# The first fourteen operands of a quarter-block product loaded straight into their remainder tiles

## The chip, the cores and the metric

The kernel runs on one core of a Trainium2 chip, as one program. The metric is the device time of one execution in microseconds (us). Three executions of the kernel before are shown, and one more under the profiler; all times of engines and queues come from that profiled one.

## What is computed

One layer of a hybrid decoder for a sequence of 2048 tokens of width 1024, in fp32. The part that matters here is its second half, an MLP of hidden width 4096 between two residual steps:

```python
h = x * (1.0 + sc2) + sh2
f = jnp.square(jax.nn.relu(h @ w_mlp_in[l])) @ w_mlp_out[l]
x = _layer_norm(DEEPNORM_ALPHA * x + (1.0 + g2) * f, ln2_g[l], ln2_b[l])
```

The first half (a gated causal convolution, a multi-scale pooling, an output projection and a norm) comes ahead of it and isn't touched.

## The kernel before, in words

**Precision.** Every fp32 operand is cut in two: a high part in fp32r, written by ScalarE (`split`, L86), and a remainder, the operand minus its high part, written by VectorE (L87). A product takes three matmuls, high by high, high by remainder and remainder by high (`mm3`, L91 to L93). So no operand can be multiplied before both `split` instructions on it are done, ScalarE's first.

**Blocks.** The 2048 rows are worked in two halves (`b` = 0 and 1) of `T` = 1024. Large products are made by the seven-product scheme on 2 by 2 blocks. In `mlp`, `up` runs over eight groups `g` of 512 hidden channels; the left operands of all of them are the same 14 pieces `B`, kept in 28 tiles of the tag `h` (high part and remainder of each), while the weights come through tiles of the tags `r` and `w`. Each of the seven products of a group reads two pieces of `B`, that is, four `h` tiles. The results of a group are stored to DRAM (`usum`). `down` then multiplies them with the second weight, in steps over products and halves of the groups.

**The quarter-block product.** For `b` = 1 (`DEEPER`) one of `down`'s seven products, A12 by B21, is split once more into seven products of quarter blocks. Its left operands are `usum[g, 1]` and the sums of its quarters, `udeep[g]`; its right operands are `wdeep[g]`, the weight's quarters and their sums. All of these lie in DRAM by then: `wdeep` is written while `up` runs (`sum_deep`, L972), `usum` and `udeep` at the end of each group (`closed`, L1060). `deep_operands(g)` (L1204) loads four pieces for each of the eight groups: 128x1024 of `usum` into an `r` tile, 128x1024 of `wdeep` into a `w` tile, 128x768 of `udeep` into an `r` tile and 128x768 of `wdeep` into a `w` tile. Each is then split into two `h` tiles. `deep_matmuls` (L1219) makes 42 matmuls of 128x256 for each group: seven products (`DEEP`), two row tiles, three passes. In a group the first of the seven reads the pieces 0 and 1, the second already the pieces 2 and 3. `left.pop()` (L1267) makes, between the third and the fourth group of operands, the sums that were put off for the last group of `up`; it takes one `h` tile for `s4`, and the stores of `usum` and `udeep` for group 7 follow it.

**Tiles.** The tag `h` has 28 tiles, `r` has 5, `w` has 6, all of 128x1024 and 4 bytes. A tile is given out when its first writer is due, and comes free when its last reader is done. At the end of `up`, `r` and `w` tiles still hold weights of the last group, and all 28 `h` tiles hold `B`: those of a piece come free with the product that reads it last.

**Order.** The kernel doesn't set semaphores. Its instructions are ordered for each engine and each queue when it is built, by a planner that goes by the order in which they are written, by the tiles that are free, and by its own costs; the order then stands, and an engine or a queue that waits for one instruction takes none behind it. Loads go through SP's queue (`nc.sync.dma_start`), most stores through POOL's.

The lines that the change and the prediction speak of: L86 and L87 (`split`), L91 to L93 (`mm3`), L1011, L1067 and L1071 (stores of `usum` and `udeep`), L1084 and L1086 (loads of the next step of `down`), L1204 to L1213 (`deep_operands`), L1219 (`deep_matmuls`), L1232 to L1250 (`deep_sums`), L1263 to L1276 (their order).

Of the kernel before, what the change touches and what calls it, by code (L numbers as in the profile page):

```python
# [8 lines left out]
F32 = mybir.dt.float32  # L9
# [20 lines left out]
Q = 256  # L30
QUARTERS = slice(0, 256), slice(256, 512)
DEEPER = (1,)
DEEP_SUMS = (0,), (1,), (2,), (3,), (4, 5), (6, 7), (), ()
HALF_SUMS = (1, 2, 3, 3, 3, 3, 3, 0)
WARM = (5, 3, 1, 2, 2, 2)
# [13 lines left out]
def tile_hybrid_layer(ctx: ExitStack, tc: tile.TileContext, opening, xT, x, wada, win,  # L49
# [13 lines left out]
    def mk(p, shape, dt, tag, bufs):  # L63
        names[0] += 1
        return p.tile(shape, dt, name=f"{tag}_{names[0]}", tag=tag, bufs=bufs)

    def t_h(dt=F32R):
        return mk(big, [P, T], dt, "h", 28)
# [4 lines left out]
    def t_w(dt=F32R):  # L73
        return mk(big, [P, T], dt, "w", 6)
# [10 lines left out]
    def split(src, hi, lo):  # L85
        high = nc.scalar.copy(hi, src)  # L86
        return high.ins, nc.vector.tensor_tensor(lo, src, hi.bitcast(F32), op=ALU.subtract).ins  # L87
# [7 lines left out]
    def tt(out_, a, b_, op):  # L95
        return nc.vector.tensor_tensor(out_, a, b_, op=op)  # L96
# [875 lines left out]
    def sum_deep(g):  # L972
        a, e = t_o(T), t_o(T)
        nc.sync.dma_start(a, w2[g, 2])
        b11, b12, b21, b22 = (a[:, i * Q : i * Q + Q] for i in range(4))
        t2, t3, t4 = (e[:, i * Q : i * Q + Q] for i in range(3))
        tt(t3, b22, b12, ALU.subtract)
        tt(b12, b12, b11, ALU.subtract)
        tt(t2, b22, b12, ALU.subtract)
        tt(t4, b21, t2, ALU.subtract)  # L980
        nc.gpsimd.dma_start(wdeep[g][:, :T], a)
        nc.gpsimd.dma_start(wdeep[g][:, T:], e[:, : 3 * Q])
# [6 lines left out]
    def up(b, g, B):  # L989
# [62 lines left out]
        nc.scalar.activation(c21, c21, AF.Square)  # L1052
        if b not in DEEPER:
            tt(c11, c21, c11, ALU.subtract)
# [59 lines left out]
    def down(b, F, g2, close):  # L1114
        X, Y = {}, {}
        lo_, hi_ = halves
        closing = b + 1 == NB
        deeper = b in DEEPER
        steps = [(i, hf) for i in ((1, 0) if deeper else (0, 1)) + (2, 3, 5, 4, 6) for hf in range(2)]
# [84 lines left out]
        def deep_operands(g):  # L1204
            tiles = []
            for t, src, n in ((t_r, usum[g, 1], T), (lambda: t_w(F32), wdeep[g][:, :T], T),
                              (t_r, udeep[g], 3 * Q), (lambda: t_w(F32), wdeep[g][:, T:], 3 * Q)):
                r = t()
                nc.sync.dma_start(r[:, :n], src)
                hi, lo = t_h(), t_h()  # L1210
                split(r[:, :n], hi[:, :n], lo[:, :n])
                tiles.append((hi, lo))
            return tiles  # L1213
# [49 lines left out]
        if deeper:  # L1263
            tiles = {}
            for g in range(3):
                tiles[g] = deep_operands(g)
            left.pop()(t_h(F32))  # L1267
            banks = []
            for gs, ns in (((g,), range(7)) for g in range(NC)):
                for g in gs:  # L1270
                    if g + 3 < NC and g + 3 not in tiles:
                        tiles[g + 3] = deep_operands(g + 3)
                if gs[-1] == NC - 1:
                    ready = operands(2)
                deep_matmuls(banks, gs, tiles, ns)
            deep_sums(banks)  # L1276
        else:
            ready = operands(0)
# [116 lines left out]
    def mlp(b, B, back, g2):  # L1395
# [15 lines left out]
        for g in range(NC):  # L1411
# [4 lines left out]
            del sums[:HALF_SUMS[g]]  # L1416
            if b in DEEPER:
                for n in DEEP_SUMS[g]:
                    sum_deep(n)
# [69 lines left out]
```

## Time and profile before

| | |
|---|---|
| time, median of 3 runs (lowest to highest) | 1735.71 us (1734.92 to 1739.76) |
| the profiled execution's own time | 1735.93 us |
| its span, first to last instruction | 1734.2 us |
| mean granted TensorE clock | 0.999 of full speed |
| TensorE busy, matmuls | 1724.6 us, 99% |
| weight loads, beside them | 1436.3 us, 83% |
| VectorE busy | 1313.6 us, 76% |
| ScalarE busy | 868.4 us, 50% |
| DMA, mean over the span | 268 GB/s |

A share over 1700 us says little about a change to one stage. Matmuls are pipelined, so where TensorE loses time is read from the distance between the starts of two matmuls, and from what the profile says each waited for. For the queues and the other engines the order of time in the stage counts: when a load was issued and when its data were there, when a split could start, and what the engine did before.

### The profile page before, as it was taken

The numbers are of one execution on the slowest core, as the hardware profiler recorded it, in microseconds if no ns is written. First come the engines' busy times: TensorE is split into PE (matmuls) and PEld (weight loads), VectorE is DVE, ScalarE is ACT, GpSimd is POOL, SyncE is SP. The second block draws the span as 40 slices with busy tenths as digits, with TensorE's granted clock in tenths as the row PEclk, the third lists the DMA queues.
The fourth block names the chain that finished last, engine by engine and source line by source line (L and its number), as shares of the span: only waits on it lengthen the run. The fifth ranks groups of instructions, "written<-read, shape, count | busy, mean of one in ns | idle before, by whom it ended". The sixth has DMA issues, their size and how long they took to land.

```text
span 1734.2 us, 21910 instructions
## 1 busy us (share of the span) xinstructions
PE 1724.6 (99%) x7855; PEld 1436.3 (83%) x7855; DVE 1313.6 (76%) x1726; ACT 868.4 (50%) x1172; POOL 205.0 (12%) x399
## 2 busy tenths in 40 slices
PE   9999999999999999999999999999999999999998
PEld 8888888888888888888888888888888889888887
DVE  8897798877777676759686789697566759665796
ACT  6322358554454554436573345765445567444451
POOL 0222220122322000100000000102111110000000
PEclk9999999999999999999999999999999999999999
DMA  9998777778888998887572265657545579777771
GB/s 387 345 340 318 300 268 269 257 268 330 317 326 317 384 419 328 309 279 278 191 266 85 99 232 217 226 190 283 205 177 221 209 260 418 308 281 258 253 265 49
DMA packets 142685, 465.24 MB, mean 268 GB/s; under 512 B 16488, under 2 KB 17008, under 8 KB 142576
## 3 DMA queue, kind: packets, MB, share of 16 engines
q1 hardware_dynamic: 97920, 303.39, 47.8%
q0 software_dynamic: 44656, 160.46, 24.3%
q8 instruction: 61, 1.00, 0.2%
q14 instruction: 48, 0.39, 0.1%
HBM read 318.55 MB, written 145.23 MB: 267 GB/s over the span
## 4 chain that ended last, share of the span: by engine, by line
PE 97%; DMA 1%; DVE 1%; issue 0%; ACT 0%; DVEq 0%; SPq 0%; ACTq 0%
PE ps L92 31%; PE ps L91 31%; PE ps L93 31%; PE ps L423 3%; DMA w<-wdeep 1%; PE ps L771 1%; DVE h L87 0%; PE ps L147 0%; DVE h L198 0%; PE ps L125 0%; ACT h L86 0%; DVE o L96 0%; DVE o L1359 0%; DVE o L1365 0%; DVEq L1485 0%
## 5 line engine op out<-in xcount | busy, mean ns | idle before, releaser
L92 PE MATMUL ps<-h,w 128*128 128x512 f32 x1312 | 510.3, 389 | 0.0
L93 PE MATMUL ps<-h,w 128*128 128x512 f32 x1312 | 510.1, 389 | 0.0
L91 PE MATMUL ps<-h,w 128*128 128x512 f32 x1312 | 510.0, 389 | 0.0
L92 PE MATMUL ps<-h,h 128*128 128x512 f32 (+1 forms) x1176 | 444.3, 378 | 0.9 <-DVE h L87 0.8
L91 PE MATMUL ps<-h,h 128*128 128x512 f32 (+1 forms) x1176 | 444.1, 378 | 0.0
L93 PE MATMUL ps<-h,h 128*128 128x512 f32 (+1 forms) x1176 | 444.1, 378 | 0.0
L86 ACT CAST h<-r 128x1024 fp32r<-128x1024 f32 (+1 forms) x192 | 193.4, 1012 | 298.8 <-PE ps L92 185.6
L87 DVE TENSOR_TENSOR h<-r,h 128x1024 fp32r<-128x1024 f32 (+1 forms) x192 | 223.7, 1170 | 98.0 <-ACT h L86 97.5
L86 ACT CAST w<-r 128x1024 fp32r<-128x1024 f32 x156 | 164.3, 1053 | 250.0 <-PE ps L92 242.7
L92 PEld LDWEIGHTS ps<-h,w 128*128 128x128 f32 x1312 | 246.2, 188 | 51.4 <-DVE h L87 0.5
L93 PEld LDWEIGHTS ps<-h,w 128*128 128x128 f32 x1312 | 246.3, 188 | 51.3
L91 PEld LDWEIGHTS ps<-h,w 128*128 128x128 f32 x1312 | 246.0, 188 | 51.4 <-issue 0.3
L87 DVE TENSOR_TENSOR w<-r,w 128x1024 fp32r<-128x1024 f32 x156 | 190.4, 1221 | 103.7 <-ACT w L86 103.0
L92 PEld LDWEIGHTS ps<-h,h 128*128 128x128 f32 x1176 | 221.2, 188 | 42.4 <-DVE h L87 1.5
L93 PEld LDWEIGHTS ps<-h,h 128*128 128x128 f32 x1176 | 221.2, 188 | 40.8
L91 PEld LDWEIGHTS ps<-h,h 128*128 128x128 f32 x1176 | 221.3, 188 | 40.8
L96 DVE TENSOR_TENSOR o<-o,o 128x1024 f32<-128x1024 f32 (+2 forms) x193 | 171.0, 890 | 41.0 <-DMA usum<-o 33.6
L96 DVE TENSOR_TENSOR o<-o,ps 128x512 f32<-128x512 f32 (+1 forms) x175 | 113.5, 658 | 52.8 <-PE ps L93 51.8
L87 DVE TENSOR_TENSOR h<-w,h 128x1024 fp32r<-128x1024 f32 x120 | 144.0, 1200 | 6.1 <-ACT h L86 5.9
L86 ACT CAST h<-w 128x1024 fp32r<-128x1024 f32 x120 | 124.3, 1036 | 14.5 <-DMA w<-wdeep 5.5
L1011 POOL DMA_DIRECT2D usum<-o x111 | 59.2, 534 | 476.9 <-ACT o L1008 218.4
L96 DVE TENSOR_TENSOR r<-r,r 128x1024 f32<-128x1024 f32 x60 | 73.4, 1223 | 21.0 <-DMA r<-in_w 15.7
(158 smaller groups left out, 1219.3 us busy)
## 6 DMA issues: line engine op xcount, KB each, us to landing
r<-usum SPq DMA_DIRECT2D x112, 512.0 KB, 5.7
usum<-o POOLq DMA_DIRECT2D x111, 512.0 KB, 4.8
w<-w2sum SPq DMA_DIRECT2D x64, 512.0 KB, 6.2
r<-in_w SPq DMA_DIRECT2D x60, 512.0 KB, 5.9
w<-in_w SPq DMA_DIRECT2D x40, 512.0 KB, 6.7
o<-in_w SPq DMA_DIRECT2D x72, 256.0 KB, 6.4
w2sum<-o POOLq DMA_DIRECT2D x64, 256.0 KB, 6.8
msum<-o POOLq DMA_DIRECT2D x18, 512.0 KB, 4.2
```

What stands on the lines that cost most here:

```text
L86: high = nc.scalar.copy(hi, src)
L87: return high.ins, nc.vector.tensor_tensor(lo, src, hi.bitcast(F32), op=ALU.subtract).ins
L91: nc.tensor.matmul(ps, whi, xhi, start=first, stop=False, skip_group_check=goes_on)
L92: nc.tensor.matmul(ps, whi, xlo, start=False, stop=False, skip_group_check=goes_on)
L93: nc.tensor.matmul(ps, wlo, xhi, start=False, stop=last, skip_group_check=goes_on)
L96: return nc.vector.tensor_tensor(out_, a, b_, op=op)
L423: nc.tensor.matmul(ps[m, h], wt[:, w : w + P], A[k][p // 2][:, hs], start=k == 0 and p == 0, stop=k == KD - 1 and p == 2)
L771: nc.tensor.transpose(ps[:, t * P : t * P + P], R[4 * h + t][:, k * P : k * P + P], ident)
L1011: nc.gpsimd.dma_start(usum[g, i], r)
```

## The change

For the first fourteen operands in order (all four of groups 0, 1 and 2, and the first two of group 3) no `r` or `w` tile is taken. The remainder's `h` tile is taken at the load instead, as fp32; the load writes it, ScalarE casts the high part out of it, and VectorE subtracts the high part from it in place. The eighteen operands after them go by way of `r` and `w` tiles as before.

```diff
+DIRECT = 14
@@ deep_operands
             for t, src, n in ((t_r, usum[g, 1], T), (lambda: t_w(F32), wdeep[g][:, :T], T),
                               (t_r, udeep[g], 3 * Q), (lambda: t_w(F32), wdeep[g][:, T:], 3 * Q)):
-                r = t()
+                if 4 * g + len(tiles) < DIRECT:
+                    lo, hi = t_h(), t_h()
+                    r = lo.bitcast(F32)
+                else:
+                    r = t()
                 nc.sync.dma_start(r[:, :n], src)
-                hi, lo = t_h(), t_h()
+                if 4 * g + len(tiles) >= DIRECT:
+                    hi, lo = t_h(), t_h()
                 split(r[:, :n], hi[:, :n], lo[:, :n])
                 tiles.append((hi, lo))
```

## Rows read from the trace of the kernel before

**Rows 1.** Waits of TensorE over the whole span: us in total, times, longest

```profile
PE ps L125 <- DVE o L127: 1.1, 1, 1.1
PE ps L92 <- DVE h L87: 0.8, 1, 0.8
PE ps L423 <- DVE h L394: 0.2, 1, 0.2
```

**Rows 2.** Timeline of PE, quarter-block product: start us, us, instruction, idle before

```profile
1423.34 0.28 PE L91 MATMUL ps<-h,h 128*128 128x256 f32 x1
...
1439.18 0.28 PE L91 MATMUL ps<-h,h 128*128 128x256 f32 x1
1439.42 0.39 PE L92 MATMUL ps<-h,h 128*128 128x256 f32 x1
...
1448.76 0.28 PE L91 MATMUL ps<-h,h 128*128 128x256 f32 x1
...
1449.86 0.28 PE L91 MATMUL ps<-h,h 128*128 128x256 f32 x1
1450.90 0.39 PE L92 MATMUL ps<-h,h 128*128 128x256 f32 x1 [0.76 <-DVE h L87]
...
1465.27 0.40 PE L91 MATMUL ps<-h,h 128*128 128x512 f32 x1
```

**Rows 3.** Timeline of DVE: start us, us, instruction

```profile
1432.79 1.22 DVE L96 TENSOR_TENSOR h<-o,o 128x1024 f32<-128x1024 f32 x1
...
1438.41 0.95 DVE L87 TENSOR_TENSOR h<-w,h 128x768 fp32r<-128x768 f32 x1
...
1447.88 1.23 DVE L87 TENSOR_TENSOR h<-w,h 128x1024 fp32r<-128x1024 f32 x1 [1.56 <-ACT h L86]
...
1449.89 0.95 DVE L87 TENSOR_TENSOR h<-w,h 128x768 fp32r<-128x768 f32 x1
...
1467.82 0.42 DVE L96 TENSOR_TENSOR o<-o,ps 128x256 f32<-128x256 f32 x1
```

**Rows 4.** Timeline of ACT: start us, us, instruction, idle before

```profile
1407.00 1.05 ACT L86 CAST w<-r 128x1024 fp32r<-128x1024 f32 x1 [1.91 <-PE ps L92]
...
1415.80 1.05 ACT L86 CAST h<-w 128x1024 fp32r<-128x1024 f32 x1 [0.19 <-DMA w<-wdeep]
...
1446.80 1.05 ACT L86 CAST h<-w 128x1024 fp32r<-128x1024 f32 x1 [1.74 <-DMA w<-wdeep]
```

**Rows 5.** Timeline of SP's queue: start us, us, load

```profile
1388.19 0.33 SPq L1209 DMA_DIRECT2D r<-usum  x1
...
1412.43 8.36 SPq L1209 DMA_DIRECT2D w<-wdeep  x6
...
1432.40 0.49 SPq L1209 DMA_DIRECT2D w<-wdeep  x1
...
1440.89 0.49 SPq L1209 DMA_DIRECT2D w<-wdeep  x1
1445.17 0.32 SPq L1209 DMA_DIRECT2D r<-usum  x1
```

**Rows 6.** By stretch: us, busy (x count) of each engine, PEclk, DMA share, GB/s

```profile
1390.70:1412.40 21.70, 21.70 (x97) 17.99 (x96) 9.48 (x10) 9.77 (x12) 1.60 (x3) 1.00 0.59 219
1412.40:1423.34 10.94, 10.94 (x49) 9.04 (x49) 6.92 (x8) 8.59 (x10) 0.53 (x1) 1.00 0.76 274
1423.34:1448.60 25.26, 25.26 (x210) 25.09 (x209) 21.98 (x25) 16.70 (x21) 3.20 (x6) 1.00 1.01 393
1448.60:1465.30 16.70, 15.81 (x130) 15.41 (x129) 16.18 (x18) 14.38 (x17) 0.00 (x0) 1.00 1.03 419
```

**Rows 7.** Loads of wdeep, from issue to landing

```profile
DMA to landing us min/median/max: 3.3/6.3/14.3
```

**Rows 8.** Groups of DVE instructions, 1385 to 1466 us: busy us, mean ns, idle before

```profile
L87 DVE TENSOR_TENSOR h<-r,h 128x1024 fp32r<-128x1024 f32 x11 | 13.4, 1220 | 2.2 <-ACT h L86 1.9
...
L96 DVE TENSOR_TENSOR o<-o,o 128x1024 f32<-128x1024 f32 x6 | 7.3, 1221 | 2.5 <-DMA usum<-o 2.4
```

**Rows 9.** Waits of SP's queue, 1385 to 1450 us: us in total, times, longest

```profile
SPq L1209 <- DMA usum<-o: 3.7, 1, 3.7
```

## The prediction, made before the changed kernel ran

> **What bounds the kernel now.** I read TensorE's waits over the whole span first. There are three [rows 1]: two in the opening, which the change doesn't touch, and one of 0.8 us for a `split` of VectorE. So TensorE is the bound nearly everywhere, and a change to loads can only give back what TensorE loses for want of operands.
>
> Where that is, the timeline of PE shows [rows 2]. The quarter-block product starts at 1423.34 us and the next step at 1465.27: 41.93 us for 8 x 42 = 336 matmuls. The pitch without a wait follows from the first rows: group 3's seventh matmul, the 133rd in all, starts at 1439.18, so 132 took 15.84 us, 0.120 each. 336 of them need 40.32 us; 1.6 us is lost. The rows show it in three places: 1439.18 to 1439.42 (0.1 over, and 0.1 more at the slower restart, as behind each of these waits), 1448.76 to 1449.86 (1.10 for six matmuls that need 0.72) and 1449.86 to 1450.90 (1.04 for one). They are 0.2, 0.4 and 1.0 us: group 3's fourth piece, then group 5's second and fourth. Outside this product I found no pitch that was off by over 0.1 us once the opening was past.
>
> What TensorE waited for is in VectorE's timeline [rows 3]. The three remainders end at 1438.41 + 0.95 = 1439.36, 1447.88 + 1.23 = 1449.11 and 1449.89 + 0.95 = 1450.84 us, each just ahead of the matmul. Behind the second stands ScalarE's cast at 1446.80 [rows 4], which had waited 1.74 us for a load of `wdeep`; and that load had been issued at 1432.40 [rows 5]. It took 14.3 us, the longest of the sixteen, where the median is 6.3 and the shortest 3.3 [rows 7]. The table by stretch says why [rows 6]: from 1423.34 on the DMA engines are full (share 1.01 to 1.03, 393 to 419 GB/s), and in the 21.7 us from 1390.70 they had a share of 0.59. The loads come in a lump, because `wdeep` has to go through `w` tiles: the weights of the last group sit in these, and SP issues the first six loads of `wdeep` only from 1412.43 on [rows 5], 11 us before the product begins.
>
> **The change part by part.** *Instructions.* Fourteen loads, casts and subtractions stay, with the same shapes; none is added or taken away. The subtraction now writes over its operand. No row shows `split` doing that; the nearest are VectorE's 1220 ns for 128x1024 with three tiles, and 1221 ns for its additions and subtractions among `o` tiles, some of them in place (L1044, L1045) [rows 8]. I take 0. The bounds are a saving of nothing, and 14 x 0.05 = 0.7 us of VectorE's time if in-place costs a twentieth more: it lies in a stretch in which VectorE works 9.48 of 21.70 us [rows 6]. Were that cover gone, the 0.7 us would fall on the splits of group 3 at the worst.
>
> *Tiles of the first twelve.* Groups 0 to 2 need no `r` or `w` tile. Instead each load takes an `h` tile, which comes free when a product of the last group of `up` ends. These have 24 matmuls of 512 columns; 97 take 21.70 us [rows 6], so one takes 5.4. Counted back from 1423.34, product ends lie at 1390.7, 1396.1, 1401.6, 1407.0, 1412.5 and 1417.9, four tiles at each; ScalarE's weight cast at 1407.00, released by PE [rows 4], is at one of them. By 1412.5 twenty tiles are free. Even if all fourteen loads take theirs first, six are left for high parts, and group 0 needs four. So `wdeep` can be loaded from 1391 on in place of 1412.43, and group 0 can be split while VectorE is idle: four splits are 2 x 1.22 + 2 x 0.95 = 4.3 us taken out of its later queue. In DMA bytes: the six lumped loads are 3 x 512 + 3 x 384 KB, 2.75 MB, and up to 1412.40 the engines move 219 GB/s against the 419 they reach later [rows 6], which leaves room for (419 - 219) x 21.7 us = 4.3 MB.
>
> *What this does to the three waits.* The `w` tiles that are free at 1412.5, 1417.9 and 1423.3 now go to the later operands: group 3's fourth piece, group 4's two, group 5's two, group 6's second. Group 5's second piece is the fourth of these, so it can be issued by 1423.3 at the latest, 9 us earlier than 1432.40. It was 0.4 us late; with 9 us in hand it is ready even if it again takes 14.3 us. Its fourth piece, 1.0 us late, is the fifth and moves likewise. Group 3's, 0.2 us late, was late in VectorE's queue, which has 4.3 us less ahead of it. All three go: -1.6 us.
>
> *Waits added.* SP's queue waits for TensorE at each direct load. Behind these stand only further loads for this product and the next step: from 1388.19 to 1445.17 SP issues nothing but the loads of L1209 [rows 5]. ScalarE takes the casts in order too, and a cast that waits for its load delays the copies of PSUM and the weight casts of `up` behind it. The weights have 11 us to spare: the cast at 1407.00 is for the last product, which starts at 1417.9. No wait of TensorE follows. The bounds are 0 and the price of the first rival below.
>
> *What is late next.* Group 7's operands don't hang on buffers but on `s4` at 1432.79 [rows 3], whose stores must land before SP can load them at 1445.17 [rows 5, 9]. Without the waits TensorE wants group 7 at 1458.7, 1.5 us earlier than now, and the DMA queue is emptier by then; I count no loss. Then the next step: its fourth row tile starts 18 matmuls of 0.227 us after the step, at 1463.7 + 4.1 = 1467.8, in a PSUM bank that VectorE empties until 1467.82 + 0.42 = 1468.24 [rows 3]. If that addition stays where it is, 0.4 us comes back as a new wait. It stands behind splits that move forward, so I take 0 to 0.4.
>
> *Sum*, against the profiled execution: 1735.93 - 1.6 + 0.1 = 1734.4 us. The median of the runs shown is 0.2 us lower than that execution; the same sum on it gives 1734.2. I keep 1734.4.
>
> A measurement of this kernel can tell about 0.3% from no change, 5.2 us. The whole pool of waits is 1.6 us, 0.09%.
>
> **Rivals.** *Slower: SP stands before the fourteenth load.* Through group 2 the direct loads use 24 of the 28 `h` tiles with their high parts, `s4` takes one; group 3's two direct loads and their casts need four, and three are left. If the queue's order puts the fourteenth ahead of group 3's third and fourth pieces and its tile is the missing one, SP waits until TensorE ends group 0, at 1423.34 + 42 x 0.120 = 1428.4, and all loads behind it wait too. In this trace SP does stand like that, for 3.7 us before the load at 1445.17, while a store of `usum` lands [rows 5, 9]. Group 3 is wanted at 1438.5, and cast and subtraction take 2.3 us, so the point that decides is a landing in 7.8 us. With 6.3 us nothing is lost; with 14.3 TensorE waits 6.5 us: 1735.93 - 1.6 + 6.5 = 1740.8. Against it: by then the lump is gone, and landings are long only in full stretches. The Trainium skill, in "DMA: Bandwidth & Descriptors", section "Anatomy of one DMA — SWDGE (gpsimd) path", says that DMA engines never wait on semaphores, and that the wait is the issuing sequencer's, ahead of dispatch. By that rule every direct load that is issued too early holds up the loads behind it; the trace agrees, with the 3.7 us.
>
> *A smaller loss: `s4` finds no tile.* If group 3's tiles are given out first, `s4` moves from 1432.79 at the worst to the end of group 2, 1438.5, and group 7 with it by 5.7 us; its last pieces have nothing to spare: 1735.93 - 1.6 + 5.7 = 1740.0. The end of group 0, 1428.4, is likelier, and costs nothing.
>
> *No gain.* The change doesn't do what it says: the direct loads queue behind one another, high parts find no tile, the DMA engines are full from 1423 on as before, and groups 3 and 5 stay late: 1735.7 to 1735.9. For it: from 1423.34 to 1448.60 loads and stores fill 393 GB/s. Against it: the product uses 1.79 MB for each group, 4.3 us at 419 GB/s against 5.0 us of matmuls, so what is loaded ahead isn't lost again.
>
> **How the numbers follow.** Forecast 0.72 (1734.3 to 1734.8), no gain 0.13, `s4` 0.05, SP before the fourteenth load 0.07, a gain elsewhere that no row shows 0.03. The low end is the fastest run shown with the full gain, 1734.92 - 1.6 = 1733.3. The high end, 1738.0, takes in no gain, partial losses of some 2 us, and the spread of the runs. Faster by over 0.3% needs 5.2 us where 1.6 are to be had: 0.01. Slower by as much needs nearly the full price of one of the two losses: 0.06. Within: 0.93.
>
> **What would show it.** Right: loads of `wdeep` into `h` tiles from about 1391 us, DMA share above 0.59 from there to 1412 and less than full for part of 1423 to 1448, no wait of TensorE in the quarter-block product, and 40.3 to 40.5 us from its first matmul to the next step's. Wrong: a DMA wait of SP before group 3, a wait for PSUM at the head of the next step, or the product still at 41.9 us. A time under 1733 or over 1738 would mean that something outside this product moved.

## The result, and the profile after

The change made the kernel slower by a little, where 1.3 us less were forecast: 1738.15 us median of 22 runs (1735.89 to 1740.6) against 1735.17 of 22 runs for the kernel before (1734.52 to 1739.76). The ratio is 1.0015, with a 95% interval from 1.0009 to 1.0022. That is smaller than the 0.3% that the prediction took for the least that can be told from no change, yet the interval doesn't hold 1. The median lies just above the range's high end, 1738.0.

| | before | after |
|---|---|---|
| median of the runs | 1735.17 us | 1738.15 us |
| span of the profiled execution | 1734.2 us | 1736.7 us |
| quarter-block product, first matmul to the next step's ("the stretch" below) | 41.93 us | 43.71 us |
| of which over 336 x 0.120 us | 1.6 us | 3.4 us |

(Lines of the file have moved: L86 is L88, L87 is L89, L91 to L93 are L93 to L95, the load at L1209 is at L1215.)

The timeline of PE for the changed kernel answers to [rows 2]:

```profile
1424.10 0.28 PE L93 MATMUL ps<-h,h 128*128 128x256 f32 x1
...
1434.77 0.28 PE L95 MATMUL ps<-h,h 128*128 128x256 f32 x1
1436.14 0.38 PE L93 MATMUL ps<-h,h 128*128 128x256 f32 x1 [1.09 <-ACT h L88]
1437.26 0.39 PE L94 MATMUL ps<-h,h 128*128 128x256 f32 x1 [0.74 <-DVE h L89]
...
1441.44 0.28 PE L95 MATMUL ps<-h,h 128*128 128x256 f32 x1
1441.73 0.50 PE L93 MATMUL ps<-h,h 128*128 128x256 f32 x2
1442.46 0.50 PE L93 MATMUL ps<-h,h 128*128 128x256 f32 x2 [0.23 <-ACT h L88]
1442.99 0.39 PE L94 MATMUL ps<-h,h 128*128 128x256 f32 x1
...
1467.81 0.40 PE L93 MATMUL ps<-h,h 128*128 128x512 f32 x1
```

The waits at 1448.76 and 1449.86 us in [rows 2], for group 5, are gone, as forecast. In their place TensorE now waits for group 2, whose operands were in time before: at 0.120 us each, 90 matmuls from 1424.10 take until 1434.90, but the next starts at 1436.14 and the one behind it at 1437.26. With a slower restart that is 2.35 us in all. Group 3 follows with 1.0 us. Behind it nothing is late.

The timeline of SP's queue (start us, us, load) shows where group 2's pieces were:

```profile
1390.06 0.33 SPq L1215 DMA_DIRECT2D h<-usum  x1
1391.42 0.32 SPq L1215 DMA_DIRECT2D h<-wdeep  x1
...
1414.51 0.42 SPq L1215 DMA_DIRECT2D h<-usum  x1
1418.62 1.21 SPq L1215 DMA_DIRECT2D w<-wdeep  x2
1419.88 0.45 SPq L1215 DMA_DIRECT2D h<-wdeep  x1
1424.06 1.80 SPq L1215 DMA_DIRECT2D w<-wdeep  x2
1425.92 0.42 SPq L1215 DMA_DIRECT2D h<-udeep  x1
1426.40 0.42 SPq L1215 DMA_DIRECT2D h<-wdeep  x1
1426.86 0.43 SPq L1215 DMA_DIRECT2D h<-usum  x1
1427.34 0.81 SPq L1215 DMA_DIRECT2D h<-wdeep  x1
```

The first direct loads come at 1390 and 1391 us, as the prediction said. But group 2's third and fourth pieces (`h<-udeep` and `h<-wdeep` at 1425.92 and 1426.40) stand behind two loads into `w` tiles at 1424.06. These belong to groups 5 and 6, whose products come 15 and 20 us behind group 2's, and they wait for `w` tiles with weights of the last group's last product, which ends at about 1424.1. SP had issued its last load before them at 1419.88. The order is fixed in the program. By their sizes in the trace and the order in which the kernel writes them, SP's loads from 1418.62 on are:

```
1418.62 w <- wdeep 128x768     group 4, fourth piece
        w <- wdeep 128x1024    group 5, second
1419.88 h <- wdeep 128x1024    group 2, second (direct)
1424.06 w <- wdeep 128x768     group 5, fourth
        w <- wdeep 128x1024    group 6, second
1425.92 h <- udeep 128x768     group 2, third (direct)
1426.40 h <- wdeep 128x768     group 2, fourth (direct)
1426.86 h <- usum 128x1024     group 3, first (direct)
1427.34 h <- wdeep 128x1024    group 3, second (direct)
```

ScalarE's timeline of the changed kernel shows when these four direct loads had landed and were cast:

```profile
1433.37 0.83 ACT L88 CAST h<-h 128x768 fp32r<-128x768 f32 x1 [5.09 <-DMA h<-udeep]
1435.26 0.83 ACT L88 CAST h<-h 128x768 fp32r<-128x768 f32 x1 [1.05 <-DMA h<-wdeep]
1437.76 1.05 ACT L88 CAST h<-h 128x1024 fp32r<-128x1024 f32 x1 [1.67 <-DMA h<-usum]
1440.63 1.05 ACT L88 CAST h<-h 128x1024 fp32r<-128x1024 f32 x1 [1.82 <-DMA h<-wdeep]
```

Group 2's are wanted at 1434.9, and the second is cast by 1436.1: TensorE starts again at 1436.14. ScalarE takes its casts in order and had stood idle for 5.09 us. Group 3's second piece, the fourteenth direct load, is cast by 1441.7, and that is group 3's 1.0 us. The four loads went out within 1.4 us and landed one behind the other, 1.9 to 2.9 us apart. So the two loads ahead cost twice here: SP stands before them, and what is behind them lands after them.

VectorE makes the remainder, and `s4` stands ahead of the one for group 2's fourth piece:

```profile
1435.11 1.22 DVE L98 TENSOR_TENSOR h<-o,o 128x1024 f32<-128x1024 f32 x1
1436.25 0.95 DVE L89 TENSOR_TENSOR h<-h,h 128x768 fp32r<-128x768 f32 x1
```

The cast ends at 1436.09, so `s4` holds this one up by 0.2 us at most; the lateness is the load's.

The table by stretch, with the stretches of [rows 6]:

```profile
1390.70:1412.40 21.70, 21.70 (x98) 17.96 (x97) 13.67 (x14) 13.21 (x17) 1.91 (x4) 1.00 0.93 334
1412.40:1423.34 10.94, 10.94 (x50) 9.07 (x49) 4.94 (x6) 5.86 (x7) 0.53 (x1) 1.00 0.91 324
1423.34:1448.60 25.26, 23.16 (x181) 21.99 (x180) 18.46 (x21) 15.37 (x19) 3.22 (x6) 1.00 0.82 300
```

The traffic moved forward as the forecast had it, from 0.59 to 0.93 of the DMA engines in the first stretch and from 1.01 to 0.82 in the third. TensorE nevertheless lost 2.1 of the 25.26 us.

The spans differ by 2.5 us and the stretch by 1.8. The other 0.7 us are one wait at 904.5 us, in the input projection. The orders of all engines and of SP's queue are the same in both kernels up to about 1388 us. Waits of 0.2 to 0.8 us at 518, 556 and 905 us stand in some profiled executions of the kernels below and not in others; the second profile of the changed kernel (e8) has none at 905 and 0.7 us at 556. So that part is not put down to the change.

### The profile page after: what moved, and what is told of

Read it like the earlier page. It is cut to its first block, busy times and chain, and to the rows that moved or that the text cites. A ratio compares the mean times of both kernels' runs of the same rounds, so it can differ in the third digit from the quotient of the medians.

```text
span 1736.7 us, 21902 instructions
## 1 busy us (share of the span) xinstructions
PE 1725.4 (99%) x7855; PEld 1436.6 (83%) x7855; DVE 1314.0 (76%) x1726; ACT 868.2 (50%) x1172; POOL 205.7 (12%) x399
## 4 chain that ended last, share of the span: by engine, by line
PE 94%; DMA 2%; DVE 2%; ACT 1%; issue 1%; SPq 0%; DVEq 0%; ACTq 0%
PE ps L93 30%; PE ps L95 30%; PE ps L94 30%; PE ps L425 3%; PE ps L773 1%; DMA h<-wdeep 1%; DVE h L89 0%; DMA r<-in_xT 0%; DMA o<-in_opening 0%; DMA r<-winsum 0%; ACT h L625 0%; DMA r<-in_wins 0%; DVE o L98 0%; DMA r<-xsum 0%; DVE o L1366 0%
## 5 line engine op out<-in xcount | busy, mean ns | idle before, releaser
L95 PE MATMUL ps<-h,w 128*128 128x512 f32 x1312 | 510.2, 389 | 0.5 <-DVE w L89 0.5
L93 PE MATMUL ps<-h,w 128*128 128x512 f32 x1312 | 510.1, 389 | 0.0
L93 PE MATMUL ps<-h,h 128*128 128x512 f32 (+1 forms) x1176 | 443.8, 378 | 1.3 <-ACT h L88 1.3
L95 PE MATMUL ps<-h,h 128*128 128x512 f32 (+1 forms) x1176 | 443.8, 378 | 0.0
L88 ACT CAST h<-r 128x1024 fp32r<-128x1024 f32 (+2 forms) x185 | 187.0, 1015 | 292.8 <-PE ps L94 179.9
L95 PEld LDWEIGHTS ps<-h,w 128*128 128x128 f32 x1312 | 246.2, 188 | 52.2 <-DVE w L89 1.0
L93 PEld LDWEIGHTS ps<-h,w 128*128 128x128 f32 x1312 | 246.0, 188 | 51.3 <-ACT h L88 0.3
L88 ACT CAST w<-r 128x1024 fp32r<-128x1024 f32 x156 | 164.6, 1055 | 246.4 <-PE ps L94 238.3
L89 DVE TENSOR_TENSOR h<-r,h 128x1024 fp32r<-128x1024 f32 (+2 forms) x185 | 216.4, 1175 | 91.3 <-ACT h L88 90.8
L89 DVE TENSOR_TENSOR w<-r,w 128x1024 fp32r<-128x1024 f32 x156 | 190.6, 1222 | 98.7 <-ACT w L88 97.8
L93 PEld LDWEIGHTS ps<-h,h 128*128 128x128 f32 x1176 | 220.9, 188 | 42.8 <-ACT h L88 1.9
L95 PEld LDWEIGHTS ps<-h,h 128*128 128x128 f32 x1176 | 221.2, 188 | 40.9
L89 DVE TENSOR_TENSOR h<-w,h 128x1024 fp32r<-128x1024 f32 (+1 forms) x113 | 136.5, 1208 | 3.8 <-ACT h L88 3.7
L88 ACT CAST h<-w 128x1024 fp32r<-128x1024 f32 (+1 forms) x113 | 117.5, 1040 | 8.6 <-DMA w<-in_w 4.1
```

The costliest lines, as they stand in the source:

```text
L93: nc.tensor.matmul(ps, whi, xhi, start=first, stop=False, skip_group_check=goes_on)
L95: nc.tensor.matmul(ps, wlo, xhi, start=False, stop=last, skip_group_check=goes_on)
```

## The experiments

Three theories stood after this. **Order**: loads that wait for a tile stand ahead of more urgent ones in SP's queue. **Tiles**: group 2's direct loads have no `h` tile before the last product ends, whatever the order. **Lump**: too many loads at once around 1424 us. The experiments e1, e2, e3 and e5 add a dependence that only fixes the order in SP's queue; e4, e6, e9 and e11 change which operands are loaded directly, and e10 and e12 do both. What is computed stays.

**e1, all later loads behind the twelfth direct one.** In the edits, `direct` is a list of the direct loads issued so far.

```diff
-                nc.sync.dma_start(r[:, :n], src)
+                at = 4 * g + len(tiles)
+                with tc.issue_after(direct[11]) if at >= DIRECT else nullcontext():
+                    load = nc.sync.dma_start(r[:, :n], src)
+                if at < DIRECT:
+                    direct.append(load.ins)
```

> The change, with every load that goes by way of an r or w tile put behind the twelfth direct load in SP's queue, so that nothing stands ahead of groups 0 to 2. Stretch = from the quarter-block product's first matmul to the next step's: 41.9 us before, 43.9 in the changed kernel, 40.3 without a wait. Theory 1 (SP's order: loads for groups 4 to 6, which wait for a w or r tile, stand ahead of group 2's direct loads): group 2's last two loads are issued at about 1418.6 us, when the sixth product of the last group ends, not at 1426; stretch 40.3 to 41.0, total 1 to 1.6 us under before. Theory 2 (h tiles: group 2's direct loads have no tile before the last product ends, whatever the order): still issued at 1424, stretch 43.9, total 2 to 3 us over before. Theory 3 (the lump: too many loads are issued at once around 1424 us and each takes long to land): here 18 loads come after 1418 in one lump, so the stretch is 43.9 or longer.

Measured: 40.31 us in the stretch, no wait in it; 1735.03 us median against 1735.45 before, ratio 0.9997 (0.9988 to 1.0006). The stretch came as the first theory had it; of its gain of 1 to 1.6 us in the total, 0.4 shows, and the interval holds 1. SP's queue in e1:

```profile
1413.14 0.32 SPq L1219 DMA_DIRECT2D h<-wdeep  x1
1417.22 0.32 SPq L1219 DMA_DIRECT2D h<-udeep  x1
1418.59 0.32 SPq L1219 DMA_DIRECT2D h<-wdeep  x1
1419.01 0.63 SPq L1219 DMA_DIRECT2D r<-udeep  x1
```

Group 2's last two loads go out at 1417.22 and 1418.59, so their tiles are there before the sixth product of the last group is over or as it ends: the theory of tiles falls. All eighteen loads into `r` and `w` tiles come after 1419 in a thicker lump, and nothing is late:

```profile
1423.34:1448.60 25.26, 25.26 (x209) 25.11 (x209) 19.74 (x22) 14.59 (x17) 3.12 (x6) 1.00 1.00 379
```

The DMA engines have a share of 1.00 in the stretch in which the changed kernel had 0.82. So the theory of the lump falls too.

**e2, only the loads into w tiles behind it; e3, only those into r tiles.**

```diff
-                with tc.issue_after(direct[11]) if at >= DIRECT else nullcontext():
+                with tc.issue_after(direct[11]) if at >= DIRECT and len(tiles) % 2 else nullcontext():
```

(e3: `len(tiles) % 2 == 0`.)

> As e1, but the loads into w tiles alone are put behind the twelfth direct load; those into r tiles stay where the changed kernel has them. Theory 1: the w tiles are what SP stood for longest (to the end of a product, 5.4 us each), so group 2 is cured: stretch 40.3 to 41.3, total 0.6 to 1.6 us under before; group 3's two direct loads still stand behind w loads. Theory 2: as the changed kernel, 43.9. Theory 3: between, 42 to 44.

> As e1, but the loads into r tiles alone are put behind the twelfth direct load; those into w tiles stay ahead. Theory 1: SP still stands for w tiles to the end of the last product before group 2's last two loads; stretch 42.5 to 44, total 1 to 3 us over before. Theory 2: 43.9. Theory 3: fewer loads before 1424, more after: 43.9 or longer.

e2: 40.49 us, 1734.57 us median, ratio 0.9997 (0.9989 to 1.0006): the stretch is as expected, and the total is 0.9 us under before, with an interval that holds 1. e3: 50.59 us, 1745.67 us median, ratio 1.0057 (1.0045 to 1.0070). Its direction was right and its size missed by 7 us: with the `w` loads still ahead, group 2's last two went out at 1425.07 and 1425.59, and group 3's pieces and group 4's, which now came behind these in the full queue, landed later still. TensorE waited 1.9 us for group 2 and 6.6 for group 3; the clock granted in 1447 to 1450 us was down to 0.50, which is part of the remaining 1.8. The loads into `w` tiles are the ones to move.

**e4, twelve direct operands.**

```diff
-DIRECT = 14
+DIRECT = 12
```

> The change with twelve direct operands in place of fourteen: group 3's first two go by way of r and w tiles. Theory 1: group 2's last two loads stand behind four w loads as in the changed kernel, so its 2.3 us of waiting stay, but group 3 is ready early: stretch 42.6 to 42.9, total about 0.5 to 1.5 us over before. Theory 2: two h tiles less are asked for, so group 2 finds its tiles: stretch 40.3 to 41. Theory 3: two loads fewer in the lump: 43 to 43.9.

Measured: 45.59 us, 1739.72 us median, ratio 1.0024 (1.0014 to 1.0033). Two direct operands less were asked for, and group 2 was no earlier: its last two loads stood behind four loads into `w` tiles again. They went out at 1424.28 and 1425.41, 1.6 and 1.0 us earlier than in the changed kernel, and landed 0.4 and 0.9 us later, so the lateness is not SP's stand alone. Group 3 was in time, as expected. The size was missed: group 2's waits were 3.9 us in place of 2.35, and 1.4 us came from the clock, which is shown in the last section.

**e5, two loads alone behind the twelfth.**

```diff
-                with tc.issue_after(direct[11]) if at >= DIRECT else nullcontext():
+                with tc.issue_after(direct[11]) if at in (23, 25) else nullcontext():
```

> The change, with two loads alone put behind the twelfth direct load in SP's queue: group 5's fourth piece and group 6's second, the two that wait for the w tiles of the last group's last product and stand ahead of group 2's last two direct loads. If SP's stand before these two is what the change costs, group 2's last two are issued at about 1420 us in place of 1426 and the quarter-block product takes 40.3 to 41.0 us to the next step (43.7 in the changed kernel), total 3 to 4 us under the changed kernel. If the loads for groups 3 to 6 that stand further ahead (r tiles at 1402 to 1411 us, w tiles at 1413 and 1418) matter too, 41.5 to 43.

Measured: 40.31 us, no wait; 1735.28 us median against 1735.04 before, ratio 1.0 (0.9991 to 1.0009). That is 0.2 us over the kernel before, where the changed kernel was 3.0 over. SP's queue in e5, and the first matmul of the stretch and the one behind it:

```profile
1419.36 0.59 SPq L1219 DMA_DIRECT2D h<-wdeep  x1
1420.01 0.58 SPq L1219 DMA_DIRECT2D h<-udeep  x1
1420.63 0.54 SPq L1219 DMA_DIRECT2D h<-wdeep  x1
1423.62 1.68 SPq L1219 DMA_DIRECT2D w<-wdeep  x2
...
1423.65 0.28 PE L93 MATMUL ps<-h,h 128*128 128x256 f32 x1
...
1463.96 0.40 PE L93 MATMUL ps<-h,h 128*128 128x512 f32 x1
```

The order is that of the changed kernel with two pairs exchanged, and the whole loss in the stretch is gone, group 3's 1.0 us with group 2's: group 2's pieces go out at 1420.01 and 1420.63, six microseconds earlier. The loads further ahead, for which SP stood at 1402 to 1418 us, cost nothing. The exchange takes away both SP's stand and the two loads' turn in landing; how much of the 3.4 us each makes is not shown.

**e6, eight direct operands** (`DIRECT = 8`).

> The change with eight direct operands: groups 0 and 1 alone. Group 2's right operands then go by way of the first two free w tiles, and nothing that is wanted later stands ahead of them. By the theory of SP's order: 40.3 to 41.0 us in the quarter-block product, total as e1 and e2, 0 to 1.5 us under before. If a direct load costs something of its own (in-place splits, SP waiting for TensorE), each of the eight still pays: 41.5 to 43.

Measured: 40.31 us, no wait; 1734.66 us median against 1735.04 before, ratio 1.0 (0.9992 to 1.0009). Eight direct loads cost the stretch nothing here, and neither do the fourteen of e1 and e5.

**e7 and e8, both kernels profiled once more.**

> The kernel before, profiled once more, to see how far its 41.9 us in the quarter-block product hold from run to run: 40.8 to 42.5. If its waits of 1.6 us were this one execution's, 40.3 to 40.6.

> The changed kernel, profiled once more: group 2's last two loads are issued at 1425 to 1427 us again (the order is fixed), and how late they are hangs on their landing: 42.5 to 47 us in the quarter-block product.

Before: 41.50 us (1.2 us of waits, for groups 3 and 5 again), 1736.05 us. After: 43.76 us, 1738.34 us, with group 2's last two loads at 1425.42 and 1425.90. Both hold in size. The kernel before waited again for the fourth pieces of groups 3 (0.9 us) and 5 (0.3), and not for group 5's second. The changed kernel waited for group 2 again, 2.0 us; group 3 was in time, as TensorE's clock had dropped and its matmuls came 1.4 us later (last section).

**e9, e10, e12, direct loads for the six pieces of wdeep of groups 0 to 2 alone.** The aim was the forecast's first half: that `wdeep` in `w` tiles makes the waits of the kernel before.

```diff
-                if 4 * g + len(tiles) < DIRECT:
+                if g < 3 and len(tiles) % 2 == 1:
...
-                if 4 * g + len(tiles) >= DIRECT:
+                if not (g < 3 and len(tiles) % 2 == 1):
```

e10 puts the later loads into `w` tiles behind the sixth direct one, e12 all later loads.

> Direct loads for the six pieces of wdeep of groups 0 to 2 alone; usum and udeep go by way of r tiles as in the kernel before. In SP's order group 2's fourth piece stands behind five loads into w tiles for groups 3 to 5, the fifth of which needs a w tile of the last product. Theory of SP's order: that one piece is issued at about 1425 us and is late as in the changed kernel: 42 to 44.5 us in the quarter-block product, total 0 to 3 us over before. If instead the lateness of the changed kernel came with loading usum and udeep directly, 40.3 to 41.

> As e9, with the loads into w tiles for the later groups put behind the sixth direct load. Theory of SP's order: group 2's last piece is issued by 1419 us; 40.3 to 40.6 us, total 0 to 1.5 us under before: the six pieces that no longer go by way of w tiles are then all that the gain needs. If the r tiles were a part of the lump, 41 to 42.

> As e10, with every load for groups 3 to 7 behind the sixth direct load, those into r tiles too. In e10 group 2's last piece was issued only at 1424.44 us, right behind a load into an r tile at 1424.03 that is wanted a group later. If that stand is what kept e10 at 41.9 us in the quarter-block product, the piece is now issued by 1419 us, group 2 has no wait, and the stretch is 40.3 to 40.9; total 0 to 1.5 us under before. If VectorE's queue in this arrangement (usum and udeep by way of r tiles, split later) is the cause, group 2's or group 4's wait stays: 41 to 42.

Measured: e9 40.67 us and 1735.04 us (ratio 1.0003, 0.9994 to 1.0012); e10 41.90 and 1735.01 (0.9999, 0.999 to 1.0009); e12 41.52 and 1735.75 (1.0002, 0.9993 to 1.0012). By the theory of SP's order all three miss in the stretch. In e9 the one piece behind the `w` loads went out at 1426.39, 1.0 us behind the product's start, and was cast by 1434.8. That is 9.4 us behind the start; in the changed kernel the fourth piece went out 2.3 us behind the start and was cast by 12.0. The 0.4 us that e9 lost are VectorE's:

```profile
1434.41 1.22 DVE L98 TENSOR_TENSOR h<-o,o 128x1024 f32<-128x1024 f32 x1
1435.54 0.95 DVE L89 TENSOR_TENSOR h<-h,h 128x768 fp32r<-128x768 f32 x1
```

Here `s4` stands ahead of a subtraction whose operands are there, and TensorE goes on at 1436.55, as that ends. Cast by 1434.8 and wanted at 1436.3, the piece had 0.6 us to spare beyond the 0.95 of its subtraction. So one urgent piece behind two waiting loads was not yet late by them. In e10 that piece went out at 1424.44, and TensorE lost 0.8 us for it and 0.8 for group 4's fourth piece. I put the first down to SP, which had stood for an `r` tile ahead of it. e12 took this stand away (the piece was out by 1419.1), and the wait stayed, 0.8 us, as the second theory of e12 had it. Group 4's wait was gone, and 0.4 us came at the end of group 0 for a copy of PSUM by ScalarE. VectorE's timeline in e12 shows what group 2's wait was:

```profile
1434.12 1.22 DVE L98 TENSOR_TENSOR h<-o,o 128x1024 f32<-128x1024 f32 x1
1435.25 0.95 DVE L89 TENSOR_TENSOR h<-h,h 128x768 fp32r<-128x768 f32 x1
```

The subtraction on group 2's fourth piece stands behind `s4` and ends at 1436.20; TensorE goes on at 1436.26. It is VectorE's order here, not SP's. In e1 and e5 `s4` stands ahead of the same subtraction, but it is over at 1429.60 and 1433.05, before TensorE wants the piece (1434.9 and 1434.5). e12 differs from e1 in `usum` and `udeep` of groups 0 to 2 going by way of `r` tiles, so their direct loads count too: with them VectorE is done with the earlier splits sooner.

**e11, direct loads for usum and udeep of groups 0 to 2 alone** (`len(tiles) % 2 == 0` in both lines above).

> Direct loads for the six pieces of usum and udeep of groups 0 to 2 alone; wdeep goes by way of w tiles as before. The w tiles stay the narrow place and the direct loads stand between loads that wait for them: group 1's udeep is issued only after the splits of group 0 have given back two w tiles, at about 1422 to 1425 us, for a product that is wanted at 1429. By both the theory of SP's order and the argument that w tiles make the lump: 43 to 48 us, total 1 to 6 us over before. If any direct load helped, 40.3 to 41.5.

Measured: 49.56 us, 1744.04 us median, ratio 1.0052 (1.0037 to 1.0067). Group 1's `udeep` went out at 1425.45, behind three loads into `w` tiles from 1423.17 on, and TensorE stood 4.3 us for its cast. It is the same fault, one group earlier, where less time is left. The size was missed: group 1's `wdeep` was 1.3 us late too, and behind the long wait 19 matmuls ran at half the clock, some 1.7 us.

## Why the prediction was wrong

**What bounds the kernel**: right. The waits in the quarter-block product recur (e7), and three variants (e1, e5, e6) bring the stretch to 40.31 us, 336 times 0.120. That they come from loads is shown by this; the small waits at 518, 556 and 905 us, which come and go, were not in the trace that was read.

**Tiles of the first twelve, and the traffic**: right. `h` tiles come free from 1390 us on, the DMA share rises to 0.93, the waits for group 5 go, and so does the one for group 3's fourth piece. That group 2's loads could have gone out at 1417 to 1419 us is shown by e1.

**In-place splits at 0**: right. They take 1225 ns in the changed kernel, where the nearest rows had 1220 and 1221 [rows 8], and e1 and e5 have fourteen of them with no wait in the stretch. In VectorE's groups between 1385 and 1466 us:

```profile
L89 DVE TENSOR_TENSOR h<-h,h 128x1024 fp32r<-128x1024 f32 x8 | 9.8, 1225 | 8.1 <-ACT h L88 8.1
```

**The step that failed** is the one on waits added: "Behind these stand only further loads for this product and the next step", costed at nothing. The runs showed 3.4 us in its place, 2.35 for group 2 and 1.0 for group 3. I looked at what kind of load stands behind a direct load, and not at how soon each is wanted, nor at what stands ahead of one. The same paragraphs had the other half of it: the `w` tiles that come free at 1423.3 "now go to the later operands", counted there as a gain of 9 us for group 5. Those loads wait for exactly these tiles, and a queue that takes its loads in order stands until they come free. Before, no urgent load was behind such a wait, because group 2's own pieces were the ones that waited for `w` tiles. With `w` tiles given over to groups 3 to 6 and group 2 moved to `h` tiles, two loads that nobody needs for 25 us hold up two that are wanted in 11, counted from 1424.06. e5 shows that these two are all of it.

**A row read wrongly.** The median of 6.3 us to landing in [rows 7] is not that of the loads: the view took in the sixteen stores of `wdeep` as well. With SP's issues alone it says:

```profile
L1209 SPq DMA_DIRECT2D w<-wdeep x16: 319/383/542, 1412.4 to 1448.6; - x16
DMA to landing us min/median/max: 3.3/8.2/14.3
```

So the loads' median was 8.2 us, above the 7.8 that decided the rival of the fourteenth load. "With 6.3 us nothing is lost" was too kind, and so was its 0.07. A smaller slip: 1792 KB for each group are 1.84 MB in the units of the sum above it, and 4.4 us at 419 GB/s; nothing hangs on it.

**The rivals**: the slower rival had the mechanism (SP stands before a load, and everything behind it waits) but the wrong loads: the fourteenth direct load in front of groups 3 and later, at 0.07, with a price of 6.5 us when landings are long. What came was loads of groups 5 and 6 in front of group 2, with 3.4 us. The fourteenth load has a part in that, the 1.0 us of group 3: it went out at 1427.34 without a stand of its own and took 13.2 us to land, the last of the line. The `s4` of the other rival moved from 1432.79 to 1435.11 us, and group 7 was not late. The slower rival's rule from the Trainium skill ("DMA: Bandwidth & Descriptors", section "Anatomy of one DMA — SWDGE (gpsimd) path"), that the issuing sequencer does the waiting, agrees with this trace: SP issued nothing from 1420.3 to 1424.06 us, while the tiles for the direct loads next in line were free or about to be, as e1's issues at 1417.22 and 1418.59 show.

**The sum.** The gain of 1.6 us was worked from one profiled execution and set against runs without a profile. In those, e1, e2, e5 and e6, which have 0.0 to 0.2 us of waits left in the stretch, lie between 0.9 us under the kernel before and 0.2 over it by their medians. Their intervals hold 1 and reach down to ratios of 0.9988 to 0.9992, which is 1.4 to 2.1 us under it. Why 1.2 to 1.6 us of waits under the profiler are not plain in the medians stays open. The two profiled executions of the kernel before (1735.93 and 1736.05 us) lie above its medians, which would fit waits that are shorter when nothing is recorded; but of the four variants, e5's lies under its median (1734.62), e1's and e6's are at theirs, and e2's is 1.0 us above its own. No run here shows the stretch without the profile. So no version was shown to be faster than the kernel before.

## What to carry to other kernels

Before giving transfers new buffers, write down the queue's new order, and for each load ask what stands ahead of it and what that one waits for: buffers that an urgent load gives up go to loads that can wait, and these then stand in its way. In a queue that takes its loads in order, put them in the order in which they are wanted, if need be by hand, and then look at the next engine's order, as `s4` in e12 shows. And read a gain of one or two microseconds from several executions, not from one.

## What the runs showed of the hardware

TensorE's clock can fall after short waits. In the second profile of the changed kernel (e8) two waits of 0.84 and 0.61 us came close together, and in the table by stretch the granted clock behind them is about half, the lower of its two levels, 1.2 GHz:

```profile
1424.00:1434.00 10.00, 10.00 (x86) 10.00 (x85) 7.64 (x9) 5.10 (x7) 2.14 (x4) 1.00 0.89 315
1434.00:1437.00 3.00, 1.55 (x11) 1.15 (x10) 2.88 (x4) 0.83 (x1) 0.53 (x1) 0.99 1.04 423
1437.00:1440.50 3.50, 3.50 (x19) 3.50 (x19) 1.23 (x1) 1.44 (x2) 0.53 (x1) 0.52 1.03 421
```

The first profile of the same kernel, with waits of 1.09 and 0.74 us, kept the full clock:

```profile
1434.00:1437.00 3.00, 1.43 (x10) 1.03 (x9) 2.76 (x3) 1.04 (x2) 0.37 (x1) 1.00 1.03 420
1437.00:1440.50 3.50, 3.24 (x27) 3.24 (x28) 1.76 (x3) 1.05 (x1) 0.70 (x2) 1.00 1.02 420
```

Behind the drop, matmuls of 128x256 start 0.21 us apart in place of 0.12 for some 16 matmuls: 1.4 us that stand in no row of waits. In e4 the same happened behind a wait of 2.65 us. So two waits of 1.45 us together slowed the matmuls by 1.4 us in one execution, and two of 1.83 together by nothing in another. (In e8 group 3's operands landed meanwhile, so that its 1.0 us of waits fell away, and the two stretches are as long as each other, 43.76 and 43.71 us.) The runs without a profile fit this: the ten runs of the changed kernel with a mean granted clock of 0.997 or 0.998 take 1739.1 us on average, the twelve with 0.999 take 1737.4. That is likely one reason why they spread over 4.7 us (1735.89 to 1740.6).

A load of 512 KB took 13.2 us to land (group 3's second piece, issued at 1427.34), where the quickest of the eight loads of this kind took 4.1; the kernel before had 3.3 to 14.3 [rows 7]. This is a place in a line rather than chance: in the second profile (e8) the same load took 13.2 us again, and in both SP's loads landed in the order of their issue, the last four of the line 1.9 to 2.9 us apart, while the DMA engines had a share of 1.02 to 1.04. So the place in the queue decided more than the size.
